# Attention trunk on one core: rope scores as fp32r products of halves, the attention gate's sums moved into the first FFN, and a reordered handover

## The chip, the cores and the metric
One core of one Trainium2 chip runs the whole program. The metric is the device time of one execution in microseconds; several executions are timed and the median is given. One further execution was taken by the hardware profiler, and every time of a single instruction comes from it.

## The reference
The program computes two layers on 256 tokens of width 2048, in float32. Every sub-layer is normalised, shifted and scaled by values that depend on a condition vector `c` (adaLN), and gated before it is added back.

```python
sc = silu(c)
for i in range(2):
    shift_m, scale_m, gate_m, shift_f, scale_f, gate_f = split(sc @ mod_w[i] + mod_b[i], 6)
    if i == 1:
        kv = shared_kv(modulate(rmsnorm(x), kv_shift, kv_scale))  # latent 512 -> 16 heads of k_nope, v; one k_rope
    h = modulate(rmsnorm(x), shift_m, scale_m)
    y = pool_mixer(h) if i == 0 else mla_mixer(h, kv)
    x = x + gate_m * y
    h = modulate(rmsnorm(x), shift_f, scale_f)
    x = x + gate_f * ((silu(h @ w_gate) * (h @ w_up)) @ w_down)   # 2048 -> 5632 -> 2048
return rmsnorm(x)
```
The attention scores of a head are a sum of two products, `q_nope . k_nope` over 128 dimensions and `q_rope . k_rope` over 64; `k_rope` is one for all heads, and both rope parts are rotated by the positions. The scores are masked causally and go through a softmax.

## The kernel before
**Weights.** Each weight matrix is cut into units of 1 MB, [128, 4, 512] float32. SP issues the load into a `raw` buffer (6 of them). ACT copies the unit to fp32r, the upper half (L374), and DVE subtracts it from the original, the lower half (L376), both into `hl` buffers (6, so three units). TensorE then makes the product in three parts, upper by upper, upper by lower and lower by upper, 24 matmuls of 128x512 (L398). A unit is thus one ACT operation, one DVE operation and 24 matmuls.

**Stages.** The first layer's mixer, then the first FFN: it is begun on six chunks of 512 hidden columns while the mixer's output is still coming in (`start_ffn`), goes on with the other chunks, and has down-projections in three groups, four column blocks each (`down`), of which the last group is cut so that its last block runs inside the handover. Then the shared keys and values (`then_attention`), the 16 heads in 8 groups of two (`project_heads`, `probabilities`, `turned`, `output`), the output projection W_O and the second FFN.

**Background.** The adaLN values are sums of `mod_w` with `silu(c)`. 168 units of 1 MB are loaded by SP and multiplied and summed by DVE (L211, `Part.unit`), spread between the other work. `push` lines them up, `plan(left, units)` sets a rate so that `left` are still open after `units` weight units, `tick` is called at each weight unit and issues what the rate allows, `hold` stops the ticks until `release`. FFN0_UNITS = 95 with a rest `n_all + MLA_LATE`: 75 sums over 95 units, 0.79 per unit. The 16 sums of the attention gate (`n_mix`) are planned beside the heads with HEAD_UNITS.

**Order.** The Tile scheduler sets the order on each engine from the program and its dependences. In the handover TensorE, ACT and DVE run in the order in which the code is written (`ordered`).

**Handover.** In `then_attention` the last down-projection units (`h.old`, `products`, L407) are mixed with the first units of the key/value projection (`h.new`). For each token half and two column blocks: `piece` adds the last result to `x` (L611, L612), `norm` computes the reciprocal root (DVE L470, POOL L472), `scale` multiplies x by it (L476, DVE for block 0, POOL for block 1), `turn` transposes on TensorE (L482), `upper` rounds to fp32r on ACT (L490), `whole` makes the float32 value (L497 on DVE, L499 on ACT) and `lower` subtracts (L503).

**Rope.** `rope_start` puts the rope parts of a group of two heads, [128 = 2 x 64, 256 tokens], and a copy with the halves swapped into a `t2k` tile (L843, L845). `rope_end` multiplies them by the tables (L849, L850) and adds into the destination (L852). The rotated key lies in `krT` twice, rows 0 to 63 of plane 0 and rows 64 to 127 of plane 1 with zeros elsewhere, so that head `h` of a group takes plane `h` against the queries of both heads (L1384, L1386, float32).

```python
pe.matmul(sp[:, 0:P], lhsT=qr[:, 0:P], rhs=kr[:, 0:P], start=False, stop=True)
```

## Time and profile before
| | |
|---|---|
| median of 3 runs | 1918.96 us (1916.93 to 1919.68) |
| profiled execution | 1918.19 us, span 1916.4 us, mean granted clock 0.987 |
| TensorE busy | 1862.8 us, 97% |
| VectorE busy | 1402.7 us, 73% |
| ScalarE busy | 850.2 us, 44% |
| GpSimd busy | 26.9 us, 1% |
| DMA | 575 MB, 300 GB/s on the mean |
| first FFN's begin (`start_ffn`) | about 169 to 400 us |
| rest of the first FFN | 400 to 880 us |
| handover | 880 to 918 us |
| shared keys and values, queries | 918 to 1010 us |
| heads | 1010 to 1098 us |
| rest of W_O | 1098 to 1170 us |
| second FFN | 1170 to 1916 us |

The span is the time from the first to the last instruction that the profile shows; 1.8 us lie around it. The shares are means over stages with different limits, so each stage is read by itself. PE is TensorE, DVE VectorE, ACT ScalarE, POOL GpSimd. A float32 matmul leaves two records on PE, an fp32r matmul one.

### The profile page before, as it was taken

How to read it: one execution, taken by the hardware profiler on the slowest of the kernel's cores; microseconds unless marked ns; L12 is line 12 of the kernel's file. 1: busy time of each engine (PE TensorE's matmuls, PEld its weight loads, DVE VectorE, ACT ScalarE, POOL GpSimd, SP SyncE). 2: the span in 40 equal slices, each digit the busy share in tenths (PEclk: the TensorE clock that was granted, in tenths of full speed). 3: DMA queues.
4: the chain of work that ended last, by engine and by line, in shares of the span. 5: the costliest groups of instructions: out<-in, count | busy, mean ns of one | idle time of the engine just before them, and what ended most of it. 6: DMA issues, size and time to landing. Idle time of an engine off the chain costs nothing.

```text
span 1916.4 us, 21930 instructions
## 1 busy us (share of the span) xinstructions
PE 1862.8 (97%) x8813; PEld 1507.8 (79%) x8813; DVE 1402.7 (73%) x1391; ACT 850.2 (44%) x958; POOL 26.9 (1%) x32
## 2 busy tenths in 40 slices
...
GB/s 399 398 418 417 368 364 333 319 299 361 357 344 332 327 330 326 332 373 274 212 371 291 293 278 194 397 318 335 260 284 240 241 240 239 249 222 205 220 198 44
DMA packets 86647, 574.98 MB, mean 300 GB/s; under 512 B 10977, under 2 KB 15505, under 8 KB 18321
## 3 DMA queue, kind: packets, MB, share of 16 engines
...
q10 hardware_dynamic: 96, 0.02, 0.0%
...
## 4 chain that ended last, share of the span: by engine, by line
PE 69%; issue 22%; DMA 3%; DVE 3%; ACT 1%; SPq 0%; POOL 0%; POOLq 0%; DVEq 0%; ACTq 0%
PE ps L398 58%; DMA raw<-in_mod_w_dram 3%; PE ps L256 2%; PE ps L973 2%; PE ps L407 2%; PE ps L1288 2%; DVE raw L211 1%; PE ps L729 1%; PE ps L1197 1%; PE ps L540 0%; DMA raw<-in_mod_block_dram 0%; PE ps L196 0%; PE ps L948 0%; PE ps L770 0%; DVE hl L376 0%
## 5 line engine op out<-in xcount | busy, mean ns | idle before, releaser
L398 PE MATMUL ps<-hl,act 128*128 128x512 f32 x6744 | 1539.5, 390 | 1.9 <-DVE hl L376 1.0
L398 PEld LDWEIGHTS ps<-hl,act 128*128 128x128 f32 x6744 | 1263.0, 188 | 264.7 <-DVE hl L376 1.8
L376 DVE TENSOR_TENSOR hl<-raw,hl 128x2048 fp32r<-128x2048 f32 x289 | 661.1, 2289 | 253.2 <-ACT hl L374 252.5
L374 ACT ACTIVATE hl<-raw 128x2048 fp32r<-128x2048 f32 x289 | 553.1, 1918 | 647.8 <-PE ps L398 572.1
L211 DVE SCALAR_TENSOR_TENSOR raw<-raw,s_row 128x2048 f32<-128x2048 f32 x168 | 383.2, 2284 | 3.6 <-DMA raw<-in_mod_wt_dram 3.6
L256 PE MATMUL ps<-raw,s_strip 128*32 128x512 f32 x392 | 65.2, 760 | 34.6 <-DMA raw<-in_mod_w_dram 33.5
L698 DVE TENSOR_TENSOR act<-ps,act 128x512 f32<-128x512 f32 x96 | 64.5, 685 | 17.5 <-PE ps L398 17.5
L256 PEld LDWEIGHTS ps<-raw,s_strip 128*32 128x32 f32 x392 | 9.5, 121 | 70.0 <-DMA raw<-in_mod_w_dram 46.3
L784 DVE TENSOR_TENSOR x<-ps,x 128x512 f32<-128x512 f32 x32 | 22.1, 690 | 38.8 <-PE ps L398 38.8
L1288 PE MATMUL ps<-act,hl 128*128 128x256 f32 x384 | 49.6, 287 | 0.0
L1288 PEld LDWEIGHTS ps<-act,hl 128*128 128x128 f32 x384 | 48.3, 195 | 0.7 <-DVE act L1253 0.2
L407 PE MATMUL ps<-hl,act 128*128 128x512 f32 x192 | 47.0, 400 | 1.2 <-DVE act L503 1.2
L732 ACT ACTIVATE act<-ps 128x512 fp32r<-128x512 f32 x44 | 23.6, 594 | 50.0 <-PE ps L729 37.6
L407 PEld LDWEIGHTS ps<-hl,act 128*128 128x128 f32 x192 | 35.2, 188 | 10.7 <-ACT act L490 2.3
L263 DVE COPY t2k<-ps 128x256 f32<-128x256 f32 x4 | 1.7, 425 | 52.9 <-ACT t2k L262 52.9
L427 ACT ACTIVATE junk<-x 128x512 bf16<-128x512 f32 x23 | 14.5, 629 | 53.2 <-DVE x L612 37.6
L802 DVE TENSOR_TENSOR t2k<-ps,t2k 128x512 f32<-128x512 f32 x24 | 16.5, 689 | 28.5 <-PE ps L398 28.5
L798 ACT ACTIVATE t2k<-ps 128x512 f32<-128x512 f32 x24 | 14.2, 590 | 47.9 <-PE ps L398 47.9
L973 PEld LDWEIGHTS ps<-act,act 128*128 128x128 f32 x128 | 24.7, 200 | 11.6 <-issue 8.4
L696 ACT ACTIVATE act<-ps 128x512 f32<-128x512 f32 x32 | 19.1, 597 | 29.0 <-PE ps L398 28.8
L973 PE MATMUL ps<-act,act 128*128 128x256 f32 x128 | 31.9, 402 | 0.0
L733 DVE TENSOR_TENSOR act<-ps,act 128x512 fp32r<-128x512 f32 x44 | 28.1, 683 | 0.9 <-ACT act L732 0.9
(222 smaller groups left out, 911.6 us busy)
## 6 DMA issues: line engine op xcount, KB each, us to landing
...
```

Source lines behind the costliest of these rows:

```text
L211: dve.scalar_tensor_tensor(out=r, in0=r, scalar=1.0, in1=s_row, op0=ALU.mult, op1=ALU.mult, accum_out=self.sums[:, self.n:self.n + 1])
L256: pe.matmul(self.bank[m * STRIP:(m + 1) * STRIP, :], lhsT=weights(k), rhs=r[:, k, i, :], start=first, stop=last)
L374: hi_ins = act.activation(hi, r, AF.Copy)
L376: lo_ins = dve.tensor_tensor(out=lo, in0=r, in1=hi.bitcast(F32), op=ALU.subtract)
L398: pe.matmul(banks[tok], lhsT=t_[:, i, k, tok * P:(tok + 1) * P], rhs=w[:, k, :], start=first and n < len(part), stop=last and n >= len(ord ...
L407: pe.matmul(bank, lhsT=t_[:, i, k, tok * P:(tok + 1) * P], rhs=w[:, k, :], start=first and n == 0, stop=last and n == len(order) - 1)
L698: dve.tensor_tensor(out=part, in0=banks[tok], in1=part, op=ALU.add)
L732: act.activation(m[:, 0, :, ts_], v, AF.Copy)
L733: dve.tensor_tensor(out=m[:, 1, :, ts_], in0=v, in1=m[:, 0, :, ts_].bitcast(F32), op=ALU.subtract)
L784: dve.tensor_tensor(out=x[:, tok, js], in0=banks[tok], in1=x[:, tok, js], op=ALU.add)
L973: pe.matmul(mixed[g][:, n % 2, :], lhsT=wp[g][:, k, ns], rhs=pool_all[g // 2][:, g % 2, k, :], start=k == 0, stop=k == KL - 1)
L1288: pe.matmul(pt[:, h, :], lhsT=w(h0 + h, k), rhs=t_[:, i, k, :], start=n == 0, stop=n == 3 * KL - 1)
```

## The change
1. **Rope scores.** `rope_end` adds in place, ACT writes the fp32r upper half of the result and DVE the lower half. For the key both go into `krT`, planes 0 and 1, all 128 rows. For the queries the 128 rows of a head's stationary operand hold its 64 upper rows and its 64 lower rows. Since `krT` holds the rotated key twice, one matmul with plane 0 gives (upper + lower) of the queries by the upper key, one with plane 1 the same by the lower key. Per head there are four fp32r matmuls instead of two float32 ones. The queries' tile `o.qrT` is now a part of a `hl` tile, `rstd_b` has a tile of its own and the memset of `krT` is gone.
2. **Background.** The 16 sums of the attention gate are planned in the first FFN: 91 sums over 94 units. `hold` and `release` around the heads and HEAD_UNITS are gone; the rest before W_O is 8 sums over 9 units.
3. **Handover.** `hold` comes one column block earlier in the last down-projection. `scale` runs on DVE for both blocks. The lower half of the first new unit is made earlier, and the blocks `a1[2]` and `b0[2]` change places.
4. **Begin of the FFNs.** In block 0 of `start_ffn` the background starts two units later.

```diff
--- before.py
+++ after.py
@@ -61,12 +61,11 @@
 BEGUN = 6
 ASIDE = 5
 
-FFN0_UNITS, MLA_UNITS, HEAD_UNITS, WO_UNITS, FFN1_UNITS = 95, 4, 16, 8, 60
+FFN0_UNITS, MLA_UNITS, WO_UNITS, FFN1_UNITS = 94, 4, 9, 60
 
 KNOWN = (1, 3, 5, 7, 9, 10, 11, 12)
 
-
-LATE, MLA_LATE, WO_LATE = 3, 5, 3
+LATE, MLA_LATE = 3, 5
 
 V_C, V_NM, V_NF, V_KVIN, V_KVN, V_QN, V_PS, V_B, V_KB, V_END = 0, 16, 48, 80, 96, 100, 104, 120, 312, 344
 
@@ -473,8 +472,8 @@
 
         def scale(self, tok, j):
             self.turned[tok, j] = t2k([P, CH]), ps_t().rearrange("p (k t) -> p k t", k=KL), t2k([P, KL, P])
-            (dve if j == 0 else pool).tensor_scalar(out=self.turned[tok, j][0], in0=x[:, tok, j * CH:(j + 1) * CH],
-                                                    scalar1=self.rstd[:, tok:tok + 1], scalar2=None, op0=ALU.mult)
+            dve.tensor_scalar(out=self.turned[tok, j][0], in0=x[:, tok, j * CH:(j + 1) * CH],
+                              scalar1=self.rstd[:, tok:tok + 1], scalar2=None, op0=ALU.mult)
 
         def turn(self, tok, j):
             xr, pt, _ = self.turned[tok, j]
@@ -745,7 +744,7 @@
             for j in range(ND):
                 js = slice(j * CH, (j + 1) * CH)
                 banks = [ps_t() for _ in range(NT)]
-                if last and j == ND - 1:
+                if last and j == ND - 2:
                     hold()
                 if last and j == ND - 1:
                     weights = [w_unit(wd[c, j]) for c in g]
@@ -845,17 +844,20 @@
             act.activation(t_[r:r + HALF, 1, :], bank[r ^ HALF:(r ^ HALF) + HALF], AF.Copy)
         return t_
 
-    def rope_end(t_, dsts):
+    def rope_end(t_, splits):
+
         dve.tensor_tensor(out=t_[:, 1, :], in0=t_[:, 1, :], in1=sin_t, op=ALU.mult)
         dve.tensor_tensor(out=t_[:, 0, :], in0=t_[:, 0, :], in1=cos_t, op=ALU.mult)
-        for rows, dst in dsts:
-            dve.tensor_tensor(out=dst, in0=t_[rows, 0, :], in1=t_[rows, 1, :], op=ALU.add)
+        dve.tensor_tensor(out=t_[:, 0, :], in0=t_[:, 0, :], in1=t_[:, 1, :], op=ALU.add)
+        for rows, hi, _ in splits:
+            act.activation(hi, t_[rows, 0, :], AF.Copy)
+        for rows, hi, lo in splits:
+            dve.tensor_tensor(out=lo, in0=t_[rows, 0, :], in1=hi.bitcast(F32), op=ALU.subtract)
 
 
 
     xT = x.rearrange("p t d -> p (t d)").rearrange("p (k t) -> p k t", t=T)
-    krT = const.tile([P, 2, T], F32, name="krT")
-    rstd_b = krT[:, 0, :]
+    rstd_b = const.tile([P, T], F32, name="rstd_b")
 
 
     def sf_block(l, j, cshift, cscale):
@@ -884,7 +886,7 @@
                         begun[c][which].block(j, hT[j])
                     if n == 2 * len(begun) - 5:
                         pieces = ahead(j + 1)
-                    if todo:
+                    if todo and (j > 0 or n + 2 >= 2 * len(begun) - todo):
                         pump(1)
                         todo -= 1
                 pump(todo)
@@ -1107,9 +1109,9 @@
     for j in range(ND):
         sf_block(1, j, C_SF1, C_AF1)
     mod_part(1, 5, gate_to, "ffn1")
-    n_ffn1, n_blocks, n_mix = KD, KD // 2, KD
+    n_ffn1, n_blocks = KD, KD // 2
     n_late = n_ffn1 + LATE * n_blocks
-    n_all = n_ffn1 + ND * n_blocks + n_mix
+    n_all = n_ffn1 + ND * n_blocks
 
     hT, begun = start_ffn(0, first, hidden_T, lambda j, parts: halves_T(j, parts), ND - 1)
     plan(n_all + MLA_LATE, FFN0_UNITS)
@@ -1127,6 +1129,7 @@
         hkv, rstd = h.hT, h.rstd
         w = [w_load_of(dkv(j)) for j in range(2)]
         split_upper(w[0])
+        split_lower(w[0])
         run(h.old(0))
         h.start()
         h.piece(0)
@@ -1134,7 +1137,6 @@
         split_upper(w[1])
         h.scale(0, 0)
         h.scale(0, 1)
-        split_lower(w[0])
         fs = h.old(1)
         run(fs[:-KL])
         h.turn(0, 0)
@@ -1163,7 +1165,7 @@
         h.lower(0, 1)
         h.turn(1, 1)
         h.upper(1, 1)
-        run(b0[2], a1[2], b1[0], b1[1])
+        run(a1[2], b0[2], b1[0], b1[1])
         h.whole(1, 1, dve)
         h.lower(1, 1)
         run(b1[2])
@@ -1312,10 +1314,9 @@
     hidden_q()
 
 
-    pool.memset(krT, 0.0)
-    rope_end(kr_t, [(slice(0, ROPE), krT[0:ROPE, 0, :]), (slice(ROPE, P), krT[ROPE:P, 1, :])])
-
-    plan(n_all - n_mix - WO_LATE, HEAD_UNITS)
+    krT = const.tile([P, 2, T], F32R, name="krT")
+    rope_end(kr_t, [(slice(0, P), krT[:, 0, :], krT[:, 1, :])])
+
     cq = [ps_t() for _ in range(NT)]
     for j in range(ND):
         if len(hmx) < ND:
@@ -1343,19 +1344,19 @@
         o = Heads()
         n = HG * T
         if g % 2 == 0:
-            q_mem[0] = act_t([P, 2, n + T], F32)
-        mem = q_mem[0][:, g % 2, :]
-        o.qT = mem[:, :n].rearrange("p (h t) -> p h t", h=HG)
-        o.qrT = mem[:, n:]
+            q_mem[0] = act_t([P, 2, n], F32)
+        o.qT = q_mem[0][:, g % 2, :].rearrange("p (h t) -> p h t", h=HG)
         kT, v = kv[g * HG // KG]
         h0 = g * HG % KG
         o.kT, o.v = kT[:, h0:h0 + HG, :], v[:, :, h0 * P:(h0 + HG) * P]
         rq = raw_t([P, KL, HG * QH])
         sync.dma_start(rq, w_uq[:, g * HG * QH:(g + 1) * HG * QH].rearrange("(k p) n -> p k n", p=P))
         tick()
+
+        mems = hl_t([P, KL * HG * QH + HG * T]), hl_t([P, KL * HG * QH])
         q_h, q_l = ([t_[:, :KL * HG * NOPE].rearrange("p (k h n) -> p k h n", k=KL, h=HG),
-                     t_[:, KL * HG * NOPE:].rearrange("p (k h n) -> p k h n", k=KL, h=HG)]
-                    for t_ in (hl_t([P, KL * HG * QH]), hl_t([P, KL * HG * QH])))
+                     t_[:, KL * HG * NOPE:KL * HG * QH].rearrange("p (k h n) -> p k h n", k=KL, h=HG)] for t_ in mems)
+        o.qrT = mems[0][:, KL * HG * QH:].rearrange("p (h t) -> p h t", h=HG)
         src = rq.rearrange("p k (h n) -> p k h n", h=HG)
         with tc.high_priority(offset=100):
             for i, ns in ((1, slice(NOPE, QH)), (0, slice(0, NOPE))):
@@ -1372,18 +1373,19 @@
         head_T(o.qT, HG, lambda h, k: q_h[0][:, k, h, :], lambda h, k: q_l[0][:, k, h, :], cqT)
 
         def finish():
-            rope_end(t_, [(slice(0, P), o.qrT)])
+            a_, b_ = slice(0, ROPE), slice(ROPE, P)
+            rope_end(t_, [(a_, o.qrT[a_, 0, :], o.qrT[b_, 0, :]), (b_, o.qrT[b_, 1, :], o.qrT[a_, 1, :])])
         o.finish = finish
         return o
 
     def probabilities(o, h):
         sp = ps_t()
         kTh, qTh = o.kT[:, h, :], o.qT[:, h, :]
-        kr, qr = krT[:, h, :], o.qrT
-        pe.matmul(sp[:, 0:P], lhsT=qTh[:, 0:P], rhs=kTh[:, 0:P], start=True, stop=False)
-        pe.matmul(sp[:, 0:P], lhsT=qr[:, 0:P], rhs=kr[:, 0:P], start=False, stop=True)
-        pe.matmul(sp[:, P:3 * P], lhsT=qTh[:, P:T], rhs=kTh, start=True, stop=False)
-        pe.matmul(sp[:, P:3 * P], lhsT=qr[:, P:T], rhs=kr, start=False, stop=True)
+        qr = o.qrT[:, h, :]
+        for cols_, ts_, n in ((sp[:, 0:P], slice(0, P), P), (sp[:, P:3 * P], slice(P, T), T)):
+            pe.matmul(cols_, lhsT=qTh[:, ts_], rhs=kTh[:, :n], start=True, stop=False)
+            for i in range(2):
+                pe.matmul(cols_, lhsT=qr[:, ts_], rhs=krT[:, i, :n], start=False, stop=i == 1)
         s_ = t2k([P, 3, P])
         act.activation(s_[:, 1, :], sp[:, P:2 * P], AF.Copy, scale=SCALE)
         for b in (0, 2):
@@ -1430,11 +1432,9 @@
     pairs = H // HG
 
     act.activation(small([P, 1]), ones[:, 0:1], AF.Exp)
-    hold()
     heads = [project_heads(g) for g in range(2)]
     for o in heads:
         o.finish()
-    release(n_all - n_mix - WO_LATE, HEAD_UNITS - 8)
 
     w_o, ob = a["w_o"], []
```

The places in the instruction order on which the prediction rests are shown below. Lines of the changed kernel are mostly one lower up to line 845 and two higher in the heads; the numbers behind the names are buffers.

DVE near the end of the first FFN, from the additions of the last chunk (L802, L801 in the change) on; L376 (L375) is a lower half, L211 (L210) a background sum, L733 (L732) the transposed middle values. Before:

```order
L802 TENSOR_TENSOR t2k_5346<-ps_5350,t2k_5346 128x512
L605 TENSOR_TENSOR act_5206<-x,act_5206 128x512
L376 TENSOR_TENSOR hl_5526<-raw_5520,hl_5525 128x2048
L802 TENSOR_TENSOR t2k_5348<-ps_5351,t2k_5348 128x512
L733 TENSOR_TENSOR act_5487<-ps_5488,act_5487 128x4x128
L733 TENSOR_TENSOR act_5487<-ps_5495,act_5487 128x4x128
L733 TENSOR_TENSOR act_5502<-ps_5503,act_5502 128x4x128
L733 TENSOR_TENSOR act_5502<-ps_5510,act_5502 128x4x128
L211 SCALAR_TENSOR_TENSOR raw_5522,sums_5279<-raw_5522,s_row 128x2048
L376 TENSOR_TENSOR hl_5559<-raw_5553,hl_5558 128x2048
L211 SCALAR_TENSOR_TENSOR raw_5555,sums_5279<-raw_5555,s_row 128x2048
```

The change:

```order
L801 TENSOR_TENSOR t2k_5394<-ps_5398,t2k_5394 128x512
L604 TENSOR_TENSOR act_5250<-x,act_5250 128x512
L801 TENSOR_TENSOR t2k_5396<-ps_5399,t2k_5396 128x512
L375 TENSOR_TENSOR hl_5577<-raw_5571,hl_5576 128x2048
L732 TENSOR_TENSOR act_5553<-ps_5554,act_5553 128x4x128
L732 TENSOR_TENSOR act_5553<-ps_5561,act_5553 128x4x128
L210 SCALAR_TENSOR_TENSOR raw_5573,sums_5360<-raw_5573,s_row 128x2048
L375 TENSOR_TENSOR hl_5610<-raw_5604,hl_5609 128x2048
L210 SCALAR_TENSOR_TENSOR raw_5606,sums_5360<-raw_5606,s_row 128x2048
L610 TENSOR_TENSOR x<-ps_5569,gate_2970 128x512
L603 TENSOR_TENSOR x<-x,gate_2970 128x512
```

The lower half that stood between the two additions now stands behind both; half of the middle values have moved ahead, out of this piece.

DVE at the handover, from the last lower half of the first FFN on; L465 (L464) starts the statistics, L476 (L475) is the scale, L520 (L519) a lower half of the new unit. Before:

```order
L376 TENSOR_TENSOR hl_5762<-raw_5759,hl_5761 128x2048
L612 TENSOR_TENSOR x<-x,act_5206 128x512
L605 TENSOR_TENSOR act_5206<-x,act_5206 128x512
L211 SCALAR_TENSOR_TENSOR raw_5712,sums_5279<-raw_5712,s_row 128x2048
L465 TENSOR_REDUCE sm_5771<-ssq_5517 128x2
L466 TENSOR_SCALAR sm_5771<-sm_5771 128x2
L611 TENSOR_TENSOR x<-ps_5751,gate_3094 128x512
L612 TENSOR_TENSOR x<-x,act_5205 128x512
L470 SCALAR_TENSOR_TENSOR sm_5812<-ssq_5517,sm_5771 128x1
L476 TENSOR_SCALAR t2k_5816<-x,rstd_5772 128x512
L520 TENSOR_TENSOR hl_5776<-raw_5773,hl_5775 128x2048
L611 TENSOR_TENSOR x<-ps_5752,gate_3094 128x512
```

The change:

```order
L611 TENSOR_TENSOR x<-x,act_5250 128x512
L604 TENSOR_TENSOR act_5250<-x,act_5250 128x512
L519 TENSOR_TENSOR hl_5824<-raw_5821,hl_5823 128x2048
L464 TENSOR_REDUCE sm_5819<-ssq_5568 128x2
L465 TENSOR_SCALAR sm_5819<-sm_5819 128x2
L610 TENSOR_TENSOR x<-ps_5799,gate_2970 128x512
L611 TENSOR_TENSOR x<-x,act_5249 128x512
L469 SCALAR_TENSOR_TENSOR sm_5861<-ssq_5568,sm_5819 128x1
L475 TENSOR_SCALAR t2k_5865<-x,rstd_5820 128x512
L475 TENSOR_SCALAR t2k_5869<-x,rstd_5820 128x512
L610 TENSOR_TENSOR x<-ps_5800,gate_2970 128x512
L611 TENSOR_TENSOR x<-x,act_5250 128x512
```

The background sum ahead of the statistics is gone, the lower half of the new unit stands ahead of them, and the second scale follows the first.

DVE in the heads; L1399 (L1401) is the reciprocal of the softmax sums, L1363 (L1364) a lower half of the query weights, L849, L850, L852 (L851) the rotation, L855 in the change the lower half of the rotated queries. Before:

```order
L850 TENSOR_TENSOR t2k_7175<-t2k_7175,cos_t 128x256
L1363 TENSOR_TENSOR hl_7394<-raw_7385,hl_7393 128x1024
L1399 RECIPROCAL sm_7132<-sm_7129 128x2
L849 TENSOR_TENSOR t2k_7175<-t2k_7175,sin_t 128x256
L1401 TENSOR_SCALAR t2k_7122<-t2k_7122,sm_7132 128x256
L852 TENSOR_TENSOR act_7038<-t2k_7175 128x256
L211 SCALAR_TENSOR_TENSOR raw_7387,sums_6588<-raw_7387,s_row 128x2048
L1428 TENSOR_TENSOR act_7207<-ps_7208,act_7207 128x512
```

The change:

```order
L850 TENSOR_TENSOR t2k_7222<-t2k_7222,cos_t 128x256
L1401 RECIPROCAL sm_7185<-sm_7182 128x2
L1403 TENSOR_SCALAR t2k_7175<-t2k_7175,sm_7185 128x256
L849 TENSOR_TENSOR t2k_7222<-t2k_7222,sin_t 128x256
L851 TENSOR_TENSOR t2k_7222<-t2k_7222 128x256
L1364 TENSOR_TENSOR hl_7448<-raw_7445,hl_7447 128x512
L855 TENSOR_TENSOR hl_7203<-t2k_7222,hl_7203 64x256
L1430 TENSOR_TENSOR act_7254<-ps_7255,act_7254 128x512
L855 TENSOR_TENSOR hl_7203<-t2k_7222,hl_7203 64x256
```

The background sum is gone and two subtractions of 64 rows have come in.

## The prediction
> **What bounds the kernel now.** Line numbers are those of the kernel before. I read the page's busy times first, then the table of windows for each stage, then the timeline at each place where TensorE pauses.
>
> ```profile
> PE 1862.8 (97%) x8813; PEld 1507.8 (79%) x8813; DVE 1402.7 (73%) x1391; ACT 850.2 (44%) x958; POOL 26.9 (1%) x32
> ```
> TensorE is the bound as a whole. The other engines can only lose time at places where a half of a weight arrives late. Those places show in the windows (columns: length, busy time and count for PE, PEld, DVE, ACT, POOL; granted clock; DMA share; GB/s):
>
> ```profile
> 400.00:450.00 50.00, 50.00 (x230) 41.59 (x229) 49.06 (x49) 23.85 (x22) 0.00 (x0) 1.00 0.80 295
> 450.00:500.00 50.00, 50.00 (x222) 41.31 (x221) 40.40 (x29) 20.79 (x16) 0.70 (x1) 1.00 1.00 398
> 800.00:850.00 50.00, 50.00 (x222) 41.38 (x222) 42.95 (x35) 18.25 (x11) 0.00 (x0) 1.00 1.00 409
> 400.00:880.00 480.00, 479.85 (x2159) 398.02 (x2158) 392.77 (x313) 188.93 (x137) 0.70 (x1) 1.00 0.88 339
> 880.00:918.00 38.00, 34.61 (x157) 27.03 (x156) 33.14 (x43) 22.12 (x41) 15.28 (x8) 1.00 0.60 211
> 918.00:1010.00 92.00, 91.52 (x542) 79.97 (x541) 81.05 (x91) 69.30 (x111) 4.13 (x4) 1.00 0.81 308
> 1010.00:1098.00 88.00, 85.59 (x581) 79.18 (x580) 84.76 (x175) 71.31 (x186) 0.61 (x1) 0.98 0.78 286
> ```
> From 400 to 880 us the first FFN has almost no pause: 222 matmuls in 50 us, 0.225 us each, so 24 of them, one weight unit, take 5.4 us. The handover (880 to 918) is idle for 3.39 us and the heads (1010 to 1098) for 2.41 us at a clock of 0.98. The change can win only there, at the start of the first FFN, and through the matmuls that it makes cheaper.
>
> **Rope scores.** The heads, in TensorE's timeline and the groups of lines:
>
> ```profile
> 1043.00 3.04 PE L1288 MATMUL ps<-act,hl 128*128 128x256 f32 x24
> 1045.88 0.60 PE L1414 MATMUL ps<-t2k,act 128*128 128x256 f32 x2
> 1048.72 0.39 PE L1384 MATMUL ps<-krT,act 128*128 128x128 f32 x2
> 1048.94 0.60 PE L1385 MATMUL ps<-act,act 128*128 128x256 f32 x2
> 1049.38 0.59 PE L1386 MATMUL ps<-krT,act 128*128 128x256 f32 x2
> 1049.81 0.82 PE L1407 MATMUL ps<-con,t2k 128*128 128x128 f32 x6
> L845 ACT ACTIVATE t2k<-ps 32x256 f32<-32x256 f32 x36 | 13.5, 375 | 0.5
> L559 ACT ACTIVATE act<-t2k 128x256 fp32r<-128x256 f32 x28 | 10.5, 444 | 0.0
> L852 DVE TENSOR_TENSOR krT<-t2k 64x256 f32<-64x256 f32 x2 | 0.8, 414 | 0.0
> ```
> A float32 matmul stands as two records. Between starts the small one (L1384) occupies TensorE for 1048.94 - 1048.72 = 0.22 us, the large one (L1386) 49.81 - 49.38 = 0.43: 0.65 per head. An fp32r matmul of 256 columns (L1288) is one record of 2.88/24 = 0.12. For one of 128 columns I bound from above by one record of the float32 one, 0.11, from below by half of 0.12, 0.06, and take 0.11. The four new ones cost 2 x 0.12 + 2 x 0.11 = 0.46: 0.19 saved per head, **3.1 us of TensorE over 16 heads** (up to 4.7 by the lower bound).
>
> Per group of two heads come two ACT copies and two subtractions on 64 rows. Nearest rows: 0.375 (L845, 32 rows) and 0.444 us (L559) for a copy, 0.414 (L852) for a subtraction; I take 0.38 and 0.41. POOL's memset of krT goes, off the path.
>
> **The sums that leave the heads.**
>
> ```profile
> 1018.80:1079.50 60.70, 58.31 (x415) 55.09 (x414) 58.35 (x133) 52.22 (x142) 0.00 (x0) 0.97 0.76 274
> 1030.80:1041.50 10.70, 10.69 (x70) 10.34 (x70) 9.42 (x22) 8.49 (x23) 0.00 (x0) 0.84 0.79 278
> L211 DVE SCALAR_TENSOR_TENSOR raw<-raw,s_row 128x2048 f32<-128x2048 f32 x9 | 20.6, 2285 | 0.0
> 1027.82 2.29 DVE L211 SCALAR_TENSOR_TENSOR raw<-raw,s_row 128x2048 f32<-128x2048 f32 x1
> 1030.03 0.16 DVE L1399 RECIPROCAL sm<-sm 128x2 f32<-128x2 f32 x1
> 1030.81 0.55 PE L1407 MATMUL ps<-con,t2k 128*128 128x128 f32 x3 [1.97 <-ACT t2k L1400]
> ```
> The window from 1018.8 to 1079.5 holds seven groups; its nine background sums (the third row counts that window alone) are 20.6 us of DVE. One stands ahead of L1399, whose reciprocal ACT's L1400 and then TensorE's transposes wait for: a pause of 1.97 us, and behind it a clock of 0.84 over 10.7 us, 1.7 us more. With no sum in the heads DVE falls from 58.4 to 58.4 - 20.6 + 14 x 0.41 = 43.5. TensorE alone would fall by 7 x 0.39 = 2.7 and by its pause and slow clock (2.39 + 1.7) to 53.9. But **ACT takes over**: 52.2 + 14 x 0.38 = 57.5 us of the 60.7. So the window shortens by at most 3.2 us by this count. ACT will not be fed at every instant (0.5 us): **heads -2.7**, bounds -7.2 (TensorE's pace, with the eighth group) and +1 (the new copy and subtraction in front of the first scores delay them, 0.38 + 0.41, with nothing to cover it).
>
> The Trainium skill ("TensorE: Matmul & The Clock Gate", Part 1) says that the clock is halved after an idle window of about 3.4 us and comes back after a busy one. Here matmuls run at half speed in the stretch behind the pause, and the row's 0.84 agrees; by this rule a pause of this length can cost almost twice its own time, depending on where the window falls.
>
> **The same sums in the first FFN.** It gets 91 planned sums over 94 weight units instead of 75 over 95: 0.97 per unit instead of 0.79. Sixteen at 2.28 (L211) are 36.5 us of DVE and 16 more MB. From 400 to 880 us DVE is busy 392.8 of 480 us, 82%, which becomes 429, 89%; the DMA moves 339 GB/s, 162.7 MB, which becomes 179.5 MB, 374 GB/s, and it did 398 and 409 in two rows without a pause. On the mean both still fit. The tight place is its end, DVE's rows of the last gate and up units:
>
> ```profile
> 842.81 2.29 DVE L376 TENSOR_TENSOR hl<-raw,hl 128x2048 fp32r<-128x2048 f32 x1
> 845.01 2.29 DVE L211 SCALAR_TENSOR_TENSOR raw<-raw,s_row 128x2048 f32<-128x2048 f32 x1
> 847.22 0.08 DVE L211 DVE_READ_ACCUMULATOR raw<-raw,s_row 128x1 f32 x1
> 851.46 0.69 DVE L802 TENSOR_TENSOR t2k<-ps,t2k 128x512 f32<-128x512 f32 x1 [3.55 <-PE ps L398]
> 854.87 0.69 DVE L802 TENSOR_TENSOR t2k<-ps,t2k 128x512 f32<-128x512 f32 x1
> 855.47 2.47 DVE L733 TENSOR_TENSOR act<-ps,act 128x512 fp32r<-128x512 f32 x4
> ```
> Start to start, a lower half takes 2.20 us, a sum 2.21, a small operation 0.60. Over the 12 units before the last four, the new order has 12 lower halves, 12 sums (9 before) and 26 small operations: 26.4 + 26.5 + 15.6 = 68.5, with some tiny ones 69. TensorE needs 12 x 5.4 + 16 transposes of 0.11 = 66.6. DVE falls behind by 2.4 us, and it also waits on TensorE within the stretch (3.55 in one wait), where its time is lost; some of this its lead covers. I take **+3**, bounds 0 (the lead suffices) and +6 (2.4 plus the whole wait), and +1.7 more if the clock drops behind one of these pauses. What is late next is the lower half of the units before the handover.
>
> **The handover.**
>
> ```profile
> 892.69 6.31 PE L407 MATMUL ps<-hl,act 128*128 128x512 f32 x27
> 894.28 2.29 DVE L211 SCALAR_TENSOR_TENSOR raw<-raw,s_row 128x2048 f32<-128x2048 f32 x1
> 899.93 3.98 POOL L476 TENSOR_SCALAR t2k<-x,rstd 128x512 f32<-128x512 f32 x1
> 900.41 0.66 PE L482 MATMUL ps<-con,t2k 128*128 128x128 f32 x4 [1.41 <-DVE t2k L476]
> 903.97 0.66 PE L482 MATMUL ps<-con,t2k 128*128 128x128 f32 x4 [0.80 <-POOL t2k L476]
> 906.50 0.49 DVE L476 TENSOR_SCALAR t2k<-x,rstd 128x512 f32<-128x512 f32 x1 [0.47 <-POOL rstd L472]
> 912.88 0.50 PE L407 MATMUL ps<-hl,act 128*128 128x512 f32 x1 [1.18 <-DVE act L503]
> ```
> The hold now comes one column block earlier, so no sum runs at 894.28 and the chain L611, L612, statistics, L476, transposes starts up to 2.2 us sooner: the 1.41 goes. The second scale of each token half moves from POOL (3.98) to DVE (0.49): the 0.80 goes; nothing waits behind it on POOL until L528, and on DVE it delays the lower half L520 by 0.49. The last pause (1.18) changes its place as two blocks of matmuls are swapped. From one row's start at 0.225 each (892.69 + 27 x 0.225 = 898.8) to the next start the pauses are 1.6, 1.3 and 1.2 with smaller ones. ACT's eight operations between keep some 0.6 to 0.9 of them. I take **-3.0**, bounds -4.5 and +1 (the lower half comes late).
>
> **The start of the first FFN.**
>
> ```profile
> 179.66 3.79 PE L398 MATMUL ps<-hl,act 128*128 128x512 f32 x16
> 183.69 2.28 DVE L211 SCALAR_TENSOR_TENSOR raw<-raw,s_row 128x2048 f32<-128x2048 f32 x1
> 183.83 5.51 PE L398 MATMUL ps<-hl,act 128*128 128x512 f32 x23 [0.38 <-DVE hl L376]
> 189.92 1.43 PE L398 MATMUL ps<-hl,act 128*128 128x512 f32 x5 [0.58 <-DVE hl L376]
> ```
> In block 0 the first two sums now come two units later; a sum ahead of a late lower half is what these two waits have in front of them. By starts the first is 183.83 - (179.66 + 16 x 0.225) = 0.57, the second 0.9 less what is left of it: **-1.2**, bounds -1.5 and 0. In the shared key/value stage only 0.48 us is idle: **-0.2**, bounds -0.5 and 0.5 (seven sums at its start instead of six).
>
> **Sum:** -1.2 + 3 - 3.0 - 0.2 - 2.7 = -4.1. The profiled execution took 1918.19 (span 1916.4 and 1.8 around it), 0.8 below the median of 1918.96. From the one 1914.1, from the other 1914.9; I say **1914.3**.
>
> **Rivals.**
> *A, all cover holds.* DVE's lead swallows the new sums and the heads run at TensorE's pace: -1.2 + 0 - 3.4 - 0.2 - 7.2 = -12: 1906. For it: no pause in rows with a DMA share of 1.00 and with DVE busy 49.06 of 50 us. Against it: ACT's 57.5.
> *B, no change.* ACT's two copies per group eat the heads' gain (0 instead of -2.7) and the last units cost 4.5: -1.2 + 4.5 - 3 - 0.2 = 0: 1918.3.
> *C, slower: the first FFN loses its cover.* At nearly one sum per unit, a unit that brings two additions as well costs DVE 2.2 + 2.2 + 1.2 = 5.6 against TensorE's 5.4, so a lower half behind both additions has no lead left. Ten places in the last down-projections and chunks are such; a pause of 1 us in each is +10, with +6 at the end: -1.2 + 16 - 3 - 0.2 - 2.7 = +9: 1927. It decides once DVE's lead there is used up, and outweighs the gains once these pauses exceed 7.1 us together. Against it: 49.06 of 50 us from 400 to 450 without one.
> *D, DMA.* If no more than the present mean of 339 GB/s could be kept up over so long a stretch, the 179.5 MB would need 529 us instead of 480: near 1964. Two rows (398 and 409) contradict it.
> The Trainium skill ("Perfetto Trace Analysis", Roofline) gives 358 GB/s as a core's share of the memory when both cores of a pair use it, and about 435 GB/s for one core's 16 engines alone; by the 358 the 179.5 MB would take 501 us, an estimate of +21 from that page. The rows of 398 and 409 exceed the share, so the trace sides with the higher figure.
>
> **Chances.** Forecast 0.53 (1911 to 1917), A 0.15, B 0.15, C 0.15, D 0.02. A measurement here tells about 0.2%, 3.8 us, from no change, so the border is 1915.1. Of the forecast's 0.53, 0.38 lies below it. Faster 0.38 + 0.15 = 0.53; same 0.15 + 0.15 = 0.30; slower 0.17. The range runs from A to between B and C: 1906 to 1924.
>
> **What would show it.** Rope: pairs of fp32r records 0.11 and 0.12 apart, TensorE's busy total down by about 3 us. Heads: no L211 between 1010 and 1098, no slow clock, ACT over 95% busy; if TensorE has no pause there, A. First FFN: pauses released by DVE's lower half, only in its last 70 us, together 3 us; pauses from 440 us on mean C, and pauses released by a DMA mean D. Handover: idle time near 1 us instead of 3.39. If it comes out above 1919, the step on the first FFN was wrong.

## The result, and the profile after

The changed kernel takes **1937.81 us** (median of five runs, 1935.83 to 1938.41) against 1918.96 (five runs, 1916.93 to 1919.68): the ratio is 1.0097, 95% interval 1.0083 to 1.0110. It is slower by 19 us; 1914.3 with a range to 1924 was predicted. The profiled execution took 1936.12 us, span 1934.3, mean granted clock 0.982.

To find the place, I compared the start of the same matmul on TensorE in the two profiles, from stage to stage. Later by (us, after minus before, from each profile's start):

| stage (times of before) | predicted | measured |
|---|---|---|
| start of the first FFN, to 193 | -1.2 | +0.1 |
| rest of the first FFN, 193 to the first L407 at 888.8 | +3.0 | +8.9 |
| handover, 888.8 to 918.8 | -3.0 | -2.5 |
| shared keys and values, queries, 918.8 to 1012.5 | -0.2 | +6.1 |
| heads, 1012.5 to 1108.5 | -2.7 | +5.2 |
| W_O and second FFN, to the end | 0 | 0.0 |
| sum | -4.1 | +17.9 |

The handover went about as predicted; the first FFN, the key/value stage and the heads came out 5.9 to 7.9 us longer than predicted. The busy times and the windows of the kernel after (columns as before):

```profile
PE 1866.8 (97%) x8813; PEld 1509.8 (78%) x8813; DVE 1413.7 (73%) x1409; ACT 856.1 (44%) x975; POOL 18.5 (1%) x29
450.00:880.00 430.00, 425.00 (x1898) 349.38 (x1896) 369.37 (x288) 162.40 (x115) 0.70 (x1) 1.00 0.96 376
800.00:850.00 50.00, 48.21 (x215) 39.30 (x215) 45.98 (x40) 18.25 (x13) 0.00 (x0) 1.00 1.01 415
850.00:900.00 50.00, 47.81 (x213) 38.68 (x212) 48.98 (x46) 22.02 (x22) 0.00 (x0) 1.00 0.92 333
918.00:1010.00 92.00, 86.94 (x491) 75.08 (x490) 68.61 (x80) 65.17 (x104) 5.30 (x6) 0.98 0.66 249
1010.00:1100.00 90.00, 82.74 (x583) 77.91 (x582) 66.58 (x162) 77.23 (x198) 0.55 (x1) 0.94 0.41 143
```
TensorE is idle for longer than before: 5.0 us from 450 to 880, 5.1 in the key/value stage, 7.3 in the heads (2.4 before), there at a clock of 0.94. Of the other engines only VectorE comes near to full, from 850 to 900 us (48.98 of 50); the DMA share is 0.96 from 450 to 880 us and 1.01 from 800 to 850. TensorE's busy total, which was to fall by about 3 us, has risen by 4: a matmul at the lower clock counts as busy for longer.

**First FFN.** TensorE pauses at 484, 503, 525, 636, 681, 814, 837, 861, 879 and 889 us, mostly for 0.6 us from start to start (the rows show 0.45 of it as idle). What ACT's upper halves waited for from 440 us to the end of the stage, first in the kernel after, then in the kernel before (us in total, times, longest; lines have moved by one):

```profile
ACT hl L373 <- DMA raw<-in_ffn_down_dram: 75.4, 20, 6.7
ACT hl L373 <- DMA raw<-in_ffn_gate_dram: 56.9, 16, 8.1
```

```profile
ACT hl L374 <- PE ps L398: 146.5, 48, 4.4
ACT hl L374 <- DMA raw<-in_ffn_gate_dram: 18.8, 4, 12.1
```
Before, the upper halves waited for TensorE to free a buffer: they were as far ahead as the buffers allow. After, they wait for loads: the lead is gone. The timeline of the kernel after at one of the pauses; the last row is from the list of DMA issues, 510 to 511 us:

```profile
510.33 0.33 SPq L386 DMA_DIRECT2D raw<-in_ffn_up_dram  x1
523.67 0.60 ACT L797 ACTIVATE t2k<-ps 128x512 f32<-128x512 f32 x1 [10.95 <-PE ps L397]
524.17 1.91 ACT L373 ACTIVATE hl<-raw 128x2048 fp32r<-128x2048 f32 x1
526.12 4.17 PE L397 MATMUL ps<-hl,act 128*128 128x512 f32 x17 [0.45 <-ACT hl L373]
raw<-in_ffn_up_dram SPq DMA_DIRECT2D x1, 1024.0 KB, 6.7
```
ACT idles for 10.95 us in front of L797, the eviction of the unit that TensorE is just finishing; the upper half of the next unit (L373) stands behind it in ACT's order. Its load was issued at 510.33 and landed 6.7 us later, so the weights had lain ready since 517.0. TensorE then waits for the 1.91 us of the copy, less what it had in hand. Six of the pauses (484, 503, 525, 636, 681 and 837) are of this form: an eviction on ACT, and the copy right behind it. In the kernel before the same place reads in the other order: the upper half goes ahead of the eviction, released by TensorE.

```profile
516.96 1.92 ACT L374 ACTIVATE hl<-raw 128x2048 fp32r<-128x2048 f32 x1 [3.52 <-PE ps L398]
521.49 0.60 ACT L798 ACTIVATE t2k<-ps 128x512 f32<-128x512 f32 x1 [2.62 <-PE ps L398]
```

**Key/value stage.** The timeline of the kernel after:

```profile
969.57 2.28 DVE L210 SCALAR_TENSOR_TENSOR raw<-raw,s_row 128x2048 f32<-128x2048 f32 x1
972.12 0.16 DVE L299 TENSOR_TENSOR cols<-sums,vcol 128x16 f32<-128x16 f32 x1
972.43 0.27 PE L291 MATMUL ps<-con,cols 128*16 128x128 f32 x1 [4.61 <-DVE cols L299]
972.55 7.48 PE L1290 MATMUL ps<-act,hl 128*128 128x256 f32 x48
```
L291 transposes the gate's sums into a row. Now that these sums end in this stage, it stands in TensorE's order between two projections, and all of TensorE waits 4.61 us for the last sum. Behind it 48 matmuls of 256 columns take 7.48 us, where 48 x 0.12 = 5.8 would do: the granted clock is 0.59 from 972.4 to 976 us, which costs 1.7 us more. In this kernel the whole loss of the stage stands at this one place.

**Heads.** The timeline of the kernel after, at the first of the two long pauses:

```profile
1071.52 1.92 ACT L373 ACTIVATE hl<-raw 128x2048 fp32r<-128x2048 f32 x1
1071.68 0.87 DVE L855 TENSOR_TENSOR hl<-t2k,hl 64x256 fp32r<-64x256 f32 x2
1072.57 0.69 DVE L1392 SCALAR_TENSOR_TENSOR t2k<-ps,con 128x128 f32<-128x128 f32 x3
1073.80 0.40 ACT L1398 ACTIVATE t2k<-t2k,sm 128x128 f32<-128x128 f32 x1 [0.37 <-DVE sm L1395]
1074.70 0.47 ACT L1411 ACTIVATE t2k<-ps 128x384 f32<-128x384 f32 x1
1075.22 1.03 PE L1416 MATMUL ps<-t2k,act 128*128 128x256 f32 x2 [2.26 <-ACT t2k L1411]
1076.46 1.06 PE L1416 MATMUL ps<-t2k,act 128*128 128x256 f32 x2
1089.92 1.93 ACT L373 ACTIVATE hl<-raw 128x2048 fp32r<-128x2048 f32 x1
1094.01 1.22 PE L1416 MATMUL ps<-t2k,act 128*128 128x256 f32 x2 [3.53 <-ACT t2k L1411]
```
On ACT a whole upper half of W_O (L373, 1.92 us) stands ahead of the softmax of one head (L1398) and the eviction of the transposed scores (L1411); TensorE waits 2.26 us for the latter, and its matmuls then take nearly the double (1.06 for two, 0.60 at full clock). But what L1398 waited for last is DVE, 0.37 us beyond the copy: there the two new subtractions of the rope edit (L855, 0.87 us) stand ahead of the masks (L1392), on which the row maxima for L1398 (L1395) wait. So both a long copy and the rope edit's own operations stand in front of this softmax. The last two rows are the second pause, with another W_O copy in front. The heads were not free of sums either: two of W_O's own are in them (14 sums before), at 1075.82 and 1091.72.

**Handover.** Its three pauses have shrunk to these two:

```profile
912.23 2.56 PE L406 MATMUL ps<-hl,act 128*128 128x512 f32 x10 [0.26 <-DVE act L502]
916.35 2.56 PE L406 MATMUL ps<-hl,act 128*128 128x512 f32 x10 [0.87 <-DVE hl L519]
```

### The profile page after: what moved, and what is told of

It is laid out like the page before. It is cut to its first block, busy times and chain, and to the rows that moved or that the text cites. A ratio compares the mean times of both kernels' runs of the same rounds, so it can differ in the third digit from the quotient of the medians.

```text
span 1934.3 us, 22024 instructions
## 1 busy us (share of the span) xinstructions
PE 1866.8 (97%) x8813; PEld 1509.8 (78%) x8813; DVE 1413.7 (73%) x1409; ACT 856.1 (44%) x975; POOL 18.5 (1%) x29
## 4 chain that ended last, share of the span: by engine, by line
PE 86%; DMA 4%; ACT 4%; DVE 4%; issue 1%; SPq 0%; POOL 0%; POOLq 0%; DVEq 0%; ACTq 0%
PE ps L397 76%; DMA raw<-in_mod_w_dram 3%; PE ps L255 2%; PE ps L975 2%; PE ps L406 2%; ACT hl L373 1%; DVE raw L210 1%; PE ps L728 1%; DVE hl L375 1%; PE ps L1290 1%; PE ps L1199 1%; ACT t2k L844 1%; DMA raw<-in_ffn_gate_dram 1%; PE ps L539 0%; DMA raw<-in_mod_block_dram 0%
## 5 line engine op out<-in xcount | busy, mean ns | idle before, releaser
L375 DVE TENSOR_TENSOR hl<-raw,hl 128x2048 fp32r<-128x2048 f32 x289 | 660.7, 2288 | 247.1 <-ACT hl L373 246.9
L373 ACT ACTIVATE hl<-raw 128x2048 fp32r<-128x2048 f32 x289 | 552.8, 1917 | 620.2 <-PE ps L397 426.9
L210 DVE SCALAR_TENSOR_TENSOR raw<-raw,s_row 128x2048 f32<-128x2048 f32 x168 | 383.2, 2284 | 1.3 <-DMA raw<-in_mod_wt_dram 1.2
L697 DVE TENSOR_TENSOR act<-ps,act 128x512 f32<-128x512 f32 x96 | 64.4, 684 | 17.9 <-PE ps L397 17.8
L797 ACT ACTIVATE t2k<-ps 128x512 f32<-128x512 f32 x24 | 14.1, 590 | 57.0 <-PE ps L397 57.0
L801 DVE TENSOR_TENSOR t2k<-ps,t2k 128x512 f32<-128x512 f32 x24 | 16.6, 690 | 23.6 <-PE ps L397 23.6
L732 DVE TENSOR_TENSOR act<-ps,act 128x512 fp32r<-128x512 f32 x44 | 28.3, 681 | 0.7 <-ACT act L731 0.6
```

Of the source, the lines that this page charges most:

```text
L210: dve.scalar_tensor_tensor(out=r, in0=r, scalar=1.0, in1=s_row, op0=ALU.mult, op1=ALU.mult, accum_out=self.sums[:, self.n:self.n + 1])
L373: hi_ins = act.activation(hi, r, AF.Copy)
L375: lo_ins = dve.tensor_tensor(out=lo, in0=r, in1=hi.bitcast(F32), op=ALU.subtract)
L697: dve.tensor_tensor(out=part, in0=banks[tok], in1=part, op=ALU.add)
L732: dve.tensor_tensor(out=m[:, 1, :, ts_], in0=v, in1=m[:, 0, :, ts_].bitcast(F32), op=ALU.subtract)
```

## Experiments

Each run's own kernel before was timed on the same chip (medians 1917.4 to 1918.7). The table gives the same shifts of TensorE as above, from one profiled execution each (differences under some 3 us are not to be trusted: see the start), and the ratio of the times, except where the kernel was executed only once. The profiled execution is not always the median one: 1921.41 with a median of 1924.50 in rope alone, 1926.46 with 1922.79 in rope with POOL, 1933.58 with 1935.77 in W_O in quarters. The expectations give the loss of the first FFN as 7.6 us; by the places of this table it is 8.9.

| run | start | first FFN | handover | key/value | heads | sum | ratio (95%) |
|---|---|---|---|---|---|---|---|
| the change | +0.1 | +8.9 | -2.5 | +6.1 | +5.2 | +17.9 | 1.0097 (1.0083 to 1.0110) |
| rope alone | -1.2 | 0 | 0 | -0.1 | +4.3 | +3.0 | 1.0028 (1.0018 to 1.0037) |
| sums alone | +0.7 | +8.5 | +2.4 | +1.6 | +0.9 | +14.1 | 1.0073 (1.0057 to 1.0090) |
| handover and start | +3.3 | 0 | -2.6 | +2.2 | -0.2 | +2.7 | 1.0010 (1.0000 to 1.0019) |
| all but the sums | +1.3 | 0 | -2.6 | +2.5 | +7.0 | +8.2 | 1.0034 (1.0022 to 1.0046) |
| gate's row later | +1.6 | +8.5 | -2.5 | +3.8 | +4.8 | +16.1 | 1.0084 (1.0067 to 1.0101) |
| W_O in quarters | +1.4 | +8.1 | -2.5 | +6.4 | +2.1 | +15.5 | 1.0092 (1.0077 to 1.0107) |
| sums, a quarter of the work | +1.8 | +5.5 | -2.6 | +5.9 | +5.3 | +15.9 | one execution |
| sums, a quarter of the load | +1.8 | +16.4 | -2.6 | +6.0 | +4.8 | +26.4 | one execution |
| handover, 91 units | +1.5 | +2.6 | -2.6 | -0.1 | -1.5 | 0.0 | 1.0000 (0.9991 to 1.0008) |
| rope with POOL | +1.8 | 0 | 0 | 0 | +6.4 | +8.2 | 1.0032 (1.0019 to 1.0045) |
| both of these | +0.9 | +2.6 | -2.6 | -0.1 | +3.0 | +3.8 | 1.0023 (1.0013 to 1.0032) |
| scale and swap alone | -0.1 | 0 | -0.4 | 0 | 0 | -0.4 | 0.9999 (0.9990 to 1.0008) |

### One part at a time

The first four take parts of the change alone, or one part out. By the medians, sums alone is 14.0 us longer than its kernel before, rope alone 5.8, handover and start 1.7; together 21.4, against 18.9 for the whole change.

**Rope alone** is the kernel before with part 1 of the change.

```diff
-        for rows, dst in dsts:
-            dve.tensor_tensor(out=dst, in0=t_[rows, 0, :], in1=t_[rows, 1, :], op=ALU.add)
+        dve.tensor_tensor(out=t_[:, 0, :], in0=t_[:, 0, :], in1=t_[:, 1, :], op=ALU.add)
+        for rows, hi, _ in splits:
+            act.activation(hi, t_[rows, 0, :], AF.Copy)
+        for rows, hi, lo in splits:
+            dve.tensor_tensor(out=lo, in0=t_[rows, 0, :], in1=hi.bitcast(F32), op=ALU.subtract)
...
-        pe.matmul(sp[:, 0:P], lhsT=qr[:, 0:P], rhs=kr[:, 0:P], start=False, stop=True)
...
+            for i in range(2):
+                pe.matmul(cols_, lhsT=qr[:, ts_], rhs=krT[:, i, :n], start=False, stop=i == 1)
```

> The kernel before with the rope scores alone changed. Two theories. 'Sums': the 19 us come from the sixteen moved sums (the first FFN +7.6 us, the wait of TensorE in the key/value stage +6.5, and in the heads ACT's splits of W_O, which the scheduler puts ahead of the softmax once no sum is there, +5.4), while the rope products themselves save their 3 us. Then this one is 2 to 5 us faster than before, with the heads (1018.8 to 1079.5 before) shortened by 2 to 4. 'Rope': the copies on ACT slow the heads whatever the sums do. Then this one is 3 to 8 us slower, all of it between the first scores and the last.

Measured: 1924.50 us. The heads lose 4.3 us, though TensorE is ahead by 2 us at 1041. The timeline of this kernel at its longest pause:

```profile
1076.54 2.28 DVE L376 TENSOR_TENSOR hl<-raw,hl 128x2048 fp32r<-128x2048 f32 x1
1077.19 1.89 ACT L374 ACTIVATE hl<-raw 128x2048 fp32r<-128x2048 f32 x1
1078.74 0.16 DVE L1403 RECIPROCAL sm<-sm 128x2 f32<-128x2 f32 x1
1078.99 0.39 ACT L1404 ACTIVATE t2k<-t2k,sm 128x128 f32<-128x128 f32 x1
1079.43 1.05 PE L1411 MATMUL ps<-con,t2k 128*128 128x128 f32 x3 [2.47 <-ACT t2k L1404]
```
A W_O lower half on DVE stands ahead of the reciprocal (L1403), a W_O upper half on ACT ahead of the normalisation (L1404), and TensorE's transposes wait for that. The edit costs time by itself, even with all sums where they were; so the first theory's 2 to 5 us of gain is refuted.

**Sums alone** is the kernel before with part 2.

```diff
-FFN0_UNITS, MLA_UNITS, HEAD_UNITS, WO_UNITS, FFN1_UNITS = 95, 4, 16, 8, 60
+FFN0_UNITS, MLA_UNITS, WO_UNITS, FFN1_UNITS = 94, 4, 9, 60
...
-    n_all = n_ffn1 + ND * n_blocks + n_mix
+    n_all = n_ffn1 + ND * n_blocks
...
-    hold()
```

> The kernel before with the sixteen sums moved alone (91 sums over 94 units of the first FFN, none in the heads, 8 over 9 units of W_O). 'Sums': first FFN +6 to +9, key/value stage +5 to +7, heads between -4 and +4: 1926 to 1938 in all. 'Rope': first FFN and key/value stage the same, +12 to +15, but the heads gain 4 to 6 by themselves: 1925 to 1929.

Measured: 1932.69 us. The first FFN loses 8.5 us, nearly as in the whole change, with pauses at the same places; the handover loses 2.4, with a wait of 3.19 us for a lower half on DVE before 903.16. The heads, free of sums, win 3.7 us up to 1041 and give back 4.5 behind 1067: no gain.

**Handover and start** is the kernel before with parts 3 and 4.

```diff
-                if last and j == ND - 1:
+                if last and j == ND - 2:
                     hold()
...
-            (dve if j == 0 else pool).tensor_scalar(...
+            dve.tensor_scalar(...
...
-                    if todo:
+                    if todo and (j > 0 or n + 2 >= 2 * len(begun) - todo):
...
+        split_lower(w[0])
         run(h.old(0))
...
-        split_lower(w[0])
...
-        run(b0[2], a1[2], b1[0], b1[1])
+        run(a1[2], b0[2], b1[0], b1[1])
```

> The kernel before with the reordered handover and the two later sums at the start of the first FFN alone. Both theories: the handover gains 2.5 to 4 us as it did in the changed kernel; the start gains nothing or up to 1.2 us (in the changed kernel the two waits went, and as much was lost just ahead of them). 1914 to 1917.

Measured: 1920.41 us. The handover wins 2.6; the sums that the earlier hold pushes on cost 2.2 in the key/value stage, where TensorE now waits at 971, 976 and 1012 us. That is a miss: 1914 to 1917 was expected.

**All but the sums** is the changed kernel with part 2 undone.

```diff
-FFN0_UNITS, MLA_UNITS, WO_UNITS, FFN1_UNITS = 94, 4, 9, 60
+FFN0_UNITS, MLA_UNITS, HEAD_UNITS, WO_UNITS, FFN1_UNITS = 95, 4, 16, 8, 60
...
-    n_all = n_ffn1 + ND * n_blocks
+    n_all = n_ffn1 + ND * n_blocks + n_mix
...
+    hold()
```

> The changed kernel with the sums put back beside the heads and at the old rates; all else as changed. 'Sums': faster than before by the rope products and the handover together, 5 to 9 us, 1910 to 1914. 'Rope': the handover's 3 us less the loss in the heads, 1918 to 1924.

Measured: 1925.32 us. The first FFN is whole again (0), and of the key/value stage's 6.1 there remain 2.5. The heads lose 7.0, more than in the whole change (5.2). Rope alone, which has its sums beside the heads too, lost 4.3 there, in an execution 3 us faster than its median; so these runs do not tell whether the sums beside the heads add to the loss.

### The key/value stage and W_O

**Gate's row later:** the changed kernel, with the transposition of the attention gate's sums six weight units later in the program.

```diff
-            pending.append((0, spread))
+            pending.append((6 if name == "mla" else 0, spread))
```

> The changed kernel, in which the transposition of the attention gate's sums (TensorE, then ACT, a row in memory and POOL) is issued six weight units later. Theory: in the key/value stage only TensorE's wait for the last sum costs time (4.6 us, and the halved clock behind it 1.7). Then 5 to 7 us less than the changed kernel, 1931 to 1933. Rival: the seven sums themselves delay the lower halves there, and the wait only gathers this delay. Then less than 2 us is won.

Measured: 1934.19 us. The 4.61 us wait is gone, and the stage loses 3.8 instead of 6.1. TensorE now waits 2.11 us at another place, for the scaling of a block that it is to transpose (L529 on ACT; timeline of this kernel):

```profile
984.07 0.53 PE L539 MATMUL ps<-con,t2k 128*128 128x128 f32 x2 [2.11 <-ACT t2k L529]
```
So the transposition was the cause of that wait, but taking it away gave back only 2.3 of the stage's 6.1 us (5 to 7 were expected); the rest is work that follows late, whose own cause I did not isolate.

**W_O in quarters:** the changed kernel, with the splits of the first three W_O units in quarters, each some 0.6 us instead of 1.9.

```diff
-        hi, lo = w_unit(w_o[u, 0])
+        hi, lo = w_unit(w_o[u, 0], KL if u < 3 else 1)
```

> The changed kernel, in which the first three units of W_O are split in quarters (four operations of 128x512 on ACT and on DVE instead of one of 128x2048), so that a softmax operation waits for at most about 0.6 us behind one. Theory: the 9.4 us lost between the fourth group of heads and the last come from the 1.9 us splits of W_O that stand ahead of the softmax on ACT, and from the halved clock behind each pause. Then 5 to 9 us less than the changed kernel, 1929 to 1933. Rival: ACT is simply full with the two copies per group. Then the same or slower, since the quarters cost ACT 0.6 us more per unit.

Measured: 1935.77 us. In the profiled execution the heads lose 2.1 instead of 5.2, but that was the fastest of four; by the ratio to its own kernel before the gain is 1 us (1.0092 against 1.0097, with overlapping intervals), where 5 to 9 were expected. The timeline of this kernel shows what is in front now:

```profile
1076.78 2.29 DVE L210 SCALAR_TENSOR_TENSOR raw<-raw,s_row 128x2048 f32<-128x2048 f32 x1
1078.99 0.17 DVE L1402 RECIPROCAL sm<-sm 128x2 f32<-128x2 f32 x1
1080.25 0.39 ACT L1403 ACTIVATE t2k<-t2k,sm 128x128 f32<-128x128 f32 x1
1080.69 0.90 PE L1410 MATMUL ps<-con,t2k 128*128 128x128 f32 x3 [3.12 <-ACT t2k L1403]
```
A background sum of the W_O stage stands ahead of the reciprocal. Behind it two of the quarters and an eviction stand on ACT ahead of the normalisation (L1403), another 1.1 us. So W_O's upper halves in one piece are not the whole cause: without them other operations stand in front. That the long operations set these pauses is read from the timelines; the time of this run does not show it.

### What the sums do to the first FFN

**A quarter of the work, a quarter of the load.** Both are the changed kernel with the sums of the first FFN cut: the first reads a quarter of each loaded row, the second loads a quarter and passes over it four times. Both leave out the products of the other three quarters, so their modulation values are not right and only the times are read.

```diff
+            n = CH if cut[0] else D
-            dve.scalar_tensor_tensor(out=r, in0=r, scalar=1.0, in1=s_row, op0=ALU.mult, op1=ALU.mult,
+            dve.scalar_tensor_tensor(out=r[:, :n], in0=r[:, :n], scalar=1.0, in1=s_row[:, :n], op0=ALU.mult, op1=ALU.mult,
```

> The changed kernel with the sums of the first FFN multiplied over a quarter of their columns only (loads as they are; the modulation values are left incomplete). If DVE, by the time that it holds a buffer and stands in front of the lower halves, makes the first FFN 7.6 us longer, this falls to under 1.5 us. If the DMA does, by the extra 16 MB, 5 us or more stay.

```diff
-            sync.dma_start(r, self.w[self.tiles[self.n] * P:(self.tiles[self.n] + 1) * P, :])
+            n = CH if cut[0] else D
+            sync.dma_start(r[:, :n], self.w[self.tiles[self.n] * P:(self.tiles[self.n] + 1) * P, :n])
+            for _ in range(D // n):
```

> The changed kernel with only a quarter of the columns of the first FFN's sums loaded, and DVE going over this quarter four times (2.4 us instead of 2.3; the modulation values are left wrong). If the DMA makes the first FFN longer, the 7.6 us fall to under 1.5. If DVE does, 5 us or more stay.

The windows and waits of the first FFN, with a quarter of the work, then with a quarter of the load:

```profile
450.00:880.00 430.00, 427.09 (x1907) 351.45 (x1906) 252.07 (x287) 164.58 (x116) 0.70 (x1) 1.00 0.92 373
ACT hl L376 <- DMA raw<-in_ffn_gate_dram: 59.0, 16, 9.6
```

```profile
450.00:880.00 430.00, 419.50 (x1857) 346.74 (x1856) 402.07 (x760) 163.18 (x111) 0.70 (x1) 0.98 0.71 248
ACT hl L377 <- PE ps L401: 222.5, 67, 10.8
```
With DVE at 252 of 430 us instead of 369, 5.5 of the 8.9 us stay: the pauses of 0.6 us stand at the same places, and those at 814, 879 and 889 vanish. So DVE's time is 3.4 us of the loss. Of the 5.5 the six pauses of 0.6 make 3.7; the rest are smaller ones that I did not trace. With 248 GB/s instead of 376 the small pauses vanish, and ACT is far ahead again, waiting for TensorE. But the stage is slower still (+16.4), by new waits: the 3.3 us of a transposition of sums (at 469), 3.5 us for DVE at 764, and two more at 868. The order on the engines was another one, so that this run does not measure the loads alone.

### What could be kept

**Handover, 91 units:** the kernel before with part 3 of the change, and FFN0_UNITS lowered from 95 to 91, so that the 75 sums are through before the earlier hold (0.82 per unit instead of 0.79).

```diff
-FFN0_UNITS, MLA_UNITS, HEAD_UNITS, WO_UNITS, FFN1_UNITS = 95, 4, 16, 8, 60
+FFN0_UNITS, MLA_UNITS, HEAD_UNITS, WO_UNITS, FFN1_UNITS = 91, 4, 16, 8, 60
```

> The kernel before with the reordered handover, without the later sums at the start, and with the first FFN's 75 sums planned over 91 units instead of 95, so that the hold does not push a sum into the key/value stage. Theory: of the handover alone, 2.8 us were won at the handover, 2.0 lost in the key/value stage by the sums that the hold left over, and 1.5 lost at the start by the split that ACT put ahead of the first pieces. Without the last two this is 2 to 3.5 us faster than before, 1915 to 1917. Rival: the key/value stage loses the same 2 us because of the new order. Then it equals the kernel before within 1 us.

Measured: 1917.49 us against 1917.69, ratio 1.0000. The handover wins its 2.6 us and the key/value stage loses nothing. The first FFN gives back 2.6, with pauses of 0.61 (680, 834), again an eviction on ACT and the copy behind it, and one of 1.2 (858).

**Rope with POOL:** rope alone, with the copies and subtractions of the queries' halves on POOL.

```diff
+            if aside:
+                pool.tensor_copy(out=hi, in_=t_[rows, 0, :])
...
+            (pool if aside else dve).tensor_tensor(out=lo, in0=t_[rows, 0, :], in1=hi.bitcast(F32), op=ALU.subtract)
```

> The kernel before with the rope scores alone changed, and the copies and subtractions of the queries' halves on POOL instead of ACT and DVE. Theory A, ACT and DVE carry too much: with the two copies gone from ACT the heads are shorter than before by 2 to 4 us, 1914 to 1917. Theory B, the softmax's chain has less work of TensorE to hide behind, whichever engine makes the halves: pauses of 1 to 3 us before the transposes stay, and the heads are 2 us longer than before or more, 1920 to 1925.

Measured: 1922.79 us, 1.0032: the same as rope alone (1.0028), though ACT and DVE have two operations each less per group. POOL's subtraction is slower (1.25 us against 0.42), and TensorE waits for it twice, 0.30 us each; so the run speaks of the load on ACT and DVE, while the way to the halves became longer. Where TensorE waits, it is again for the normalised scores (timeline of this kernel):

```profile
1078.59 2.30 DVE L376 TENSOR_TENSOR hl<-raw,hl 128x2048 fp32r<-128x2048 f32 x1
1080.80 0.16 DVE L1406 RECIPROCAL sm<-sm 128x2 f32<-128x2 f32 x1
1081.00 0.40 ACT L1407 ACTIVATE t2k<-t2k,sm 128x128 f32<-128x128 f32 x1
1081.45 1.11 PE L1414 MATMUL ps<-con,t2k 128*128 128x128 f32 x3 [2.00 <-ACT t2k L1407]
```
**Both of these together,** the two diffs above with part 3, nothing new:

> The two together. The sum of what they do alone: 1911 to 1914 by theory A, 1918 to 1921 by theory B.

Measured: 1921.78 us, 1.0023. It keeps the cost of the rope scores.

**Scale and swap alone:** the kernel before with the scale on DVE for both blocks and the swap of `a1[2]` and `b0[2]`, nothing else of part 3.

```diff
-            (dve if j == 0 else pool).tensor_scalar(...
+            dve.tensor_scalar(...
...
-        run(b0[2], a1[2], b1[0], b1[1])
+        run(a1[2], b0[2], b1[0], b1[1])
```

> The kernel before with two pieces of the handover alone: both scales on DVE and the two blocks a1[2] and b0[2] exchanged; hold, lower half and everything else as before. Theory: TensorE's second wait there (0.80 on POOL's scale) goes and the one at the end shrinks by 0.3, at no cost elsewhere, since no sum changes its place: 0.8 to 1.5 us faster than before, which is less than a measurement tells. Rival: any change in the handover moves the sums and the heads' order and costs 1 to 3 us elsewhere.

Measured: 1917.84 us against 1917.82. The handover wins 0.4 us only; the other 2.2 of the 2.6 need the earlier hold or the earlier lower half, which were not taken apart. No version was found that beats the kernel before measurably.

## Why the prediction was wrong, point by point

**Rope scores on TensorE: right.** From the first matmul of one head's scores to that of the next head's, before and after (timelines):

```profile
1074.34 0.39 PE L1383 MATMUL ps<-act,act 128*128 128x128 f32 x2
1075.65 0.38 PE L1383 MATMUL ps<-act,act 128*128 128x128 f32 x2
```

```profile
1086.80 0.39 PE L1386 MATMUL ps<-act,act 128*128 128x128 f32 x2
1087.91 0.39 PE L1386 MATMUL ps<-act,act 128*128 128x128 f32 x2
```
1.31 us became 1.11: 0.20 saved per head, 3.2 us over 16 heads, as predicted (3.1). It was no gain in time.

**Heads: wrong sign (-2.7 predicted, +5.2 measured), and it was the step "ACT takes over".** It summed ACT's work and saw it fill the window. ACT is busy for 77.2 of 90 us, 86%, and not over 95%; taking the new work off it (rope with POOL) changes nothing. What paces the stage is the chain of one softmax, with small operations on ACT and DVE in turn, each of which may find an operation of 1.9 to 2.3 us in front of it (a W_O half, or a sum). TensorE has other matmuls to cover that; the rope edit makes this cover shorter. Cutting three W_O units in quarters took 3 us off the heads of one profile, but hardly any off the time, so the long operations are read from the timelines and not shown by a run of their own. That the shorter cover is what rope adds is argued from the runs with rope (+2.1 to +7.0) and those without (-1.5 to +0.9), not shown by itself: rope's own operations stand in the chain as well (L855 above), and the order of the instructions differs. A third rival does not show: the queries' halves now hold an `hl` buffer for longer, but no instruction that writes such a buffer in the heads waits for a rope matmul, in the kernel after or in rope alone. The reading of the background sum at 1027.82 as the cause of the 1.97 us pause fits: without it the heads are some 4 us ahead at 1041. But removing such sums (sums alone, +0.9) leaves W_O's halves and the later sums to stand in front instead. Nor is the bound of +1 right: it priced the new operations alone.

**First FFN: +3, bounds 0 to +7.7 with the slow clock; measured +8.9.** The step counted DVE's time over the last units. DVE accounts for 3.4 us, close to the term, but in part by luck: of the three pauses that go with DVE's work only one (889, 1.01 us idle) was released by a lower half, and the one at 814 lies outside the stretch that was counted. Missed was the larger part, 5.5: mostly, on ACT the upper half of the next unit went behind an eviction, at a rate of sums at which the upper halves no longer had a lead over TensorE. Neither DVE's count nor the mean DMA rate shows that. Moving the sums alone brings this order, so the sums cause it; why the scheduler chose it is open. Pauses did come from 484 us on, as rival C had it, but for ACT's upper halves and not for lower halves behind two additions. Of C's time (1927) 16 us were in this stage; the stage lost 8.9. D is refuted: 376 GB/s held over 430 us. The three settings that were run give 0.79 sums per unit no loss, 0.82 a loss of 2.6, 0.97 of 8.9: there was no slack to fill, even though the profile showed DVE at 82%. I did not separate the order from late landings as causes of the lost lead: at 814 us a load was in fact late.

```profile
813.87 1.91 ACT L373 ACTIVATE hl<-raw 128x2048 fp32r<-128x2048 f32 x1 [8.05 <-DMA raw<-in_ffn_gate_dram]
815.83 1.43 PE L397 MATMUL ps<-hl,act 128*128 128x512 f32 x5 [1.34 <-ACT hl L373]
```

**Key/value stage: -0.2 predicted, +6.1 measured.** The step asked how much was idle there, not what else ends there once the sums move. That was the transposition of the gate's sums, a matmul of 0.27 us that the prediction did not count at all; its wait went when it was put later, though most of the loss then came back elsewhere. The seventh sum at the start of the stage, which the prediction priced within 0.5 us, belongs to it as well: what the earlier hold pushes on cost 2.2 us by itself (handover and start).

**Handover: -3.0 predicted, -2.5 measured, right.** The chain starts sooner, and the last pauses are 0.26 and 0.87. The second scale's move from POOL to DVE was to bring 0.8 of it; by itself, with the swap, it is worth 0.4.

**Start of the first FFN: -1.2 predicted, +0.1 measured, open.** The two waits at 184 and 190 us are gone (-1.5 between 181 and 193), but 3.2 us are lost ahead of them, from 168 to 174 us. The windows, before and after, give the reason, in the clock (last columns: clock, DMA share, GB/s):

```profile
168.00:174.00 6.00, 5.04 (x24) 3.79 (x25) 4.72 (x11) 3.88 (x5) 0.00 (x0) 1.00 1.02 421
168.00:174.00 6.00, 5.78 (x13) 4.09 (x14) 4.73 (x9) 4.93 (x5) 0.00 (x0) 0.50 1.01 415
```
TensorE ran at half speed there in the kernel after and at full speed in the kernel before. Kernels without part 4 of the change show it too: in rope with POOL the clock is 0.61 in this window, +2.7 us are lost and then -1.5 won; in rope alone, with the same code up to there, it is 0.74, with +1.2 and then -1.2; in sums alone it is 1.00, and nothing is lost. So it is not part 4 that sets the clock at this place, and where TensorE is slower there the two waits go without part 4. No profile has part 4 at the full clock, so the term stays unsettled.

**The sentence "if it comes out above 1919, the step on the first FFN was wrong" held, but it was a third of the answer:** against the sum, the first FFN is 5.9 us off, the key/value stage 6.3, the heads 7.9, the start 1.3 and the handover 0.5.
